# Hybrid decoder layer: two blocks of the latent branch's output projection computed as a pair with seven-product units

## The chip, the cores and the metric

The kernel runs on one core of a Trainium2 chip. The core has a matrix engine (TensorE, in the profile PE for matmuls and PEld for weight loads), a vector engine (DVE), a scalar engine (ACT), GpSimd (POOL) and SyncE (SP); the last two here mainly issue DMA transfers, which sixteen DMA engines carry out. Every engine works through its own list of instructions in order, and waits at an instruction until the semaphores it names have been reached. The metric is the device time of one execution in microseconds. Weights and activations lie in the chip's memory (HBM) and pass through on-chip memory; matmul results accumulate in eight banks of 128 x 512 numbers, here called accumulators.

## What is computed

One decoder layer on 256 tokens of width 2048, in float32:

```python
h  = rms_norm(x)
P  = h @ w_in                       # latent q, kv | rope key | windowed q, k, v | two gates
A  = latent attention (16 heads)    # o_a, 256 x 2048
B  = windowed attention (32 heads)  # o_b, 256 x 2048
merged = sigmoid(gA) * (A @ w_o_mla) + sigmoid(gB) * (B @ w_o_swa)
y  = merged @ w_out
x  = x + rms_norm(y)
a, b = split(rms_norm(x) @ w_up)    # 2 x 5632 columns
x  = x + rms_norm((gelu(causal_conv3(a)) * b) @ w_down)
```

The change concerns `A @ w_o_mla`, a product of 256 x 2048 by 2048 x 2048.

## The kernel before

**Products.** A float32 operand is held as two parts, hi (a cast to a reduced format, made by ACT) and lo (the remainder, made by DVE). `mm3` (L195 to L197) makes one product from three matmuls: hi by hi (L195), hi by the weight's lo (L196), lo by the weight's hi (L197). A weight chunk of 128 x 1024 comes by a DMA from SP into a raw buffer (`raw`), is cast (L160, `whi`) and has its remainder taken (L161, `wlo`). Raw buffers come from a ring of three with two more in some stages (`new_raw`), or in turn from a list of places (`more_raw`).

**Plain blocks.** `gemm` makes one block of 512 columns for both halves of the tokens, with two accumulators. It goes through the 16 pieces of 128 rows (k) of the weight; a chunk holds two of them, and gives 2 x 2 products, 12 matmuls.

**Pairs.** `pair_gemm` makes two blocks of 512 columns at once for both token halves, with four accumulators c. Its work is a row of units, each of two k, written as a string: "p" is plain, eight products; "s" forms the 2 x 2 x 2 block product with seven products from sums of weights and sums of activations. Three more intermediate sums go into four further accumulators q, and `end_sums` adds these together at the end. The sums of activations (`token_sums`) are made by DVE and ACT ahead of the unit. The differences of weights are either made on the spot or beforehand: `park_sums` loads two rows of weights through POOL into a staging tile (tag "sg"), lets DVE make four subtractions (L249) and writes both results to HBM, from where `seven_parked` loads them as ordinary chunks.

**Order.** The program counts ticks, one per chunk or unit half; `at(t, f)` puts a step into tick t. A scheduler then settles the order of each engine's list from what depends on what.

**Stages around the change.** The windowed branch comes first, then its gates and its projection; latent attention (heads in eight units); the last windowed block; the four blocks of the latent gates, whose tanh values ACT makes (L1005) and POOL stores to HBM as `ta_d` (L1006); then A @ w_o_mla (`wo_a`) as four plain blocks j, each evacuated by DVE with the gates loaded back (`merge_loads`, tiles `lta` and `lyb`: L1047 and L1048) and transposed by TensorE (`m_cols`). At the start of this stage memory areas of earlier stages are given back and opened anew as areas p3, p6, px and p4; a tile there waits for all that used the place before. Behind it stand W_out (a pair w of units "ppspspsp" and two plain blocks), the residual (x is loaded anew, `late_loads`, L1029), the up columns in eleven groups, with the down product as pairs d0, d1, db and dc between and after them. The last pair, dc, leaves its second token half partly to the end (`rest`). The tail squares and sums the result, scales it, adds the residual and stores it.

In before, the differences for dc (tc0 to tc3) and one set for the pairs d (ta4) are made during latent attention, seven sets (ta) in the up groups 1 to 5, and those for db (tb) in the groups 6 to 10. The four last additions of dc (L1472: the sums of the seven-product units to the down result `dsum`, in the profile ds) are put into ticks 16 and 17 after the end of db.

Of the kernel before, what the change touches and what calls it, by code (L numbers as in the profile page):

```python
# [11 lines left out]
F32 = mybir.dt.float32  # L12
F32R = mybir.dt.float32r
# [3 lines left out]
ALU = mybir.AluOpType  # L17
AX = mybir.AxisListType

P = 128  # L20
D = 2048
S = 256
NT = 2
KT = D // P
# [18 lines left out]
def trunk_layer(ctx, tc, x, x_cols_in, conv_cols_in, g_mix_post, g_ffn_post, w_in, w_q, w_kv,  # L43
                sinks, rel, wo_a, wo_b, w_out, w_up, w_down, rope_tab, strip_sel, out):
    nc = tc.nc
    vec, act, pe, pool = nc.vector, nc.scalar, nc.tensor, nc.gpsimd
# [29 lines left out]
    def warm_up(n):  # L76
        for i in range(n):
# [6 lines left out]
                       base=0, channel_multiplier=1)  # L84
# [20 lines left out]
    flex = ["raw"]  # L105
# [22 lines left out]
    def wchunk(src, shape, own=None, rawp=None, rbufs=1, parts=None):  # L128
        i = cnt[0]
        cnt[0] += 1  # L130
        n = int(np.prod(shape))
        raw = rawp.tile([P, 1024], F32, name=f"raw{i}", tag="xraw", bufs=rbufs) if rawp else \
            new_raw(f"raw{i}")
        dst = raw[:, :n]
        if len(shape) == 2:
            dst = dst.rearrange("p (a b) -> p a b", a=shape[0])
        elif len(shape) == 3:
            dst = dst.rearrange("p (a b c) -> p a b c", a=shape[0], b=shape[1])
        if len(shape) == 3:
            for k in range(shape[0]):  # L140
                nc.sync.dma_start(dst[:, k], src[:, k])
        else:
            ins = nc.sync.dma_start(dst, src)
            if more_raw and more_raw[-1] is raw_x and "rx" not in staged:
                staged.add("rx")
                tc.keep_in_program_order(ins)
        return convert(raw, n, own=own, parts=parts)

    def convert(raw, n, own=None, parts=None, into=None):
        i = cnt[0]  # L150
        cnt[0] += 1
        if into:
            hi, lo = into
        elif own:
            hi, lo = (own.tile([P, 1024], F32R, name=f"w{part}{i}", tag="w" + part) for part in ("hi", "lo"))
        else:
            extra = in_turn("w")
            hi, lo = (ring_tile("w" + part, f"w{part}{i}", F32R, extra) for part in ("hi", "lo"))
        for a, b in parts or ((0, n),):
            act.copy(hi[:, a:b], raw[:, a:b])  # L160
            vec.tensor_tensor(lo[:, a:b], raw[:, a:b], hi[:, a:b].bitcast(F32), op=ALU.subtract)  # L161
        return hi, lo
# [14 lines left out]
    def at(t, *fs):  # L177
        steps[max(t, now[0])].extend(fs)
# [55 lines left out]
    def park_sums(name, w, k, c0, pl, tag, t0, bufs=None):  # L234

        td = [dram.tile([P, 1024], F32, name=f"{name}{i}") for i in range(2)]
        st = []

        def load():
            st.append(sb(pl, [P, D], f"{name}s", tag=tag, bufs=bufs))  # L240
            for i in range(2):
                ins = pool.dma_start(st[0][:, i * 1024:(i + 1) * 1024], w[(k + i) * P:(k + i + 1) * P, c0:c0 + 1024])
                if tag not in staged:
                    tc.keep_in_program_order(ins)
            staged.add(tag)

        def less(o, x, y):
            o, x, y = (st[0][:, i * 512:(i + 1) * 512] for i in (o, x, y))
            tc.keep_in_program_order(vec.tensor_tensor(o, x, y, op=ALU.subtract))  # L249
# [12 lines left out]
        at(t0, even)  # L262
        at(t0 + 1, odd)
        return td

    def park_a(i, pl, tag, t0, **kw):
        u, p = (i, 0) if i < NA[0] else (i - NA[0], 1)
        return park_sums(f"ta{i}_", w_down, 2 * u, 1024 * p, pl, tag, t0, **kw)
# [717 lines left out]
        at(t0 + 6, lambda: pt(0), lambda: pt(1))  # L986
        at(t0 + 7, lambda: pv(0), lambda: pv(1))

    for i in range(NB2):
        parked_b2.append(park_sums(f"tc{i}_", w_down, 24 + 2 * i, 1024, t0=now[0] + 7 + 7 * i, **STAGE))  # L990
    parked_a.append(park_a(EARLY, t0=now[0] + 7 + 7 * NB2, **STAGE))
    b = now[0] + 2
    for u in range(8):
        if u % 4 == 0:
# [26 lines left out]
    def late_loads(i):  # L1021

        if i < 4:
            if i == 0:
                gpost.append(sb(p6, [P, D], "gpost", tag="gp"))
            pool.dma_start(gpost[0][:, i * 512:(i + 1) * 512], g_mix_post[i * 512:(i + 1) * 512].partition_broadcast(P))
        else:
            t, j = divmod(i - 4, 4)
            nc.sync.dma_start(x2[t][j], x[t * P:(t + 1) * P, j * 512:(j + 1) * 512])  # L1029
# [4 lines left out]
    def m_cols(p, ld):  # L1034
        pt = pst.tile([P, 512], F32, name=f"mT{p}", tag="t")
        for i in range(2):
            for t in range(NT):
                c = (2 * (p % 2) + i) * P
                pe.transpose(pt[:, i * 256 + t * P:i * 256 + (t + 1) * P], ld[t][0][:, c:c + P], ident)
        split_to(mth[p][:, :], mtl[p][:, :], pt, 0.5)  # L1040

    def merge_loads(j):
        ld = []
        for t in range(NT):
            a = sb(p4, [P, 512], f"lta{j}_{t}", tag="lta", bufs=3)
# [4 lines left out]
        return ld  # L1050

    yg_all = [[sb(p6, [P, 1024], f"yg_{t}_{j}", tag="f" + "ab"[t], bufs=2) for j in range(2)] for t in range(NT)]
# [7 lines left out]
    for i in range(4, 12):  # L1060
        at(now[0] + 10 + 2 * i, lambda i=i: late_loads(i))
    for j in range(4):
        ld = merge_loads(j)
        if j == 2:
            for u in range(W_ORDER.count("s")):
                at(now[0] + 2 + 4 * u, lambda u=u: m_sums(u))
        acc, _ = gemm(AH, AL, wo_a, 0, KT, 512 * j, 512, ps=(pss, "s") if j == 3 else None)
        for t in range(NT):
            a, b = ld[t]
            vec.scalar_tensor_tensor(a, a, 1.0, acc[t], op0=ALU.add, op1=ALU.mult)  # L1070
            vec.tensor_tensor(a, a, b, op=ALU.add)
        for p in range(2):
            at(now[0] + (2 if j == 3 else 1) + p, lambda p=2 * j + p, ld=ld: m_cols(p, ld))


    blocks = [(0, 512), (512, 512), (1024, 512), (1536, 256), (1792, 256)]
# [186 lines left out]
    def unpark(t, j):  # L1263
        if j == 0:
            x2_all[t] = sb(p3, [P, D], f"x2b_{t}", tag=f"x2_{t}")
        c = slice(j * 512, (j + 1) * 512)
        nc.sync.dma_start(x2_all[t][:, c], x2_d[t, :, c])
# [57 lines left out]
            at(now[0] + 1 + 2 * i, lambda i=i: conv_cols(4 * c + i, sa[0][i], sa[1][i], slot0 + i))  # L1325

    es7 = ffn_up0()
    for i in range(sum(NA) - EARLY - 1):
        parked_a.append(park_a(i + EARLY + 1, t0=now[0] + 8 + 15 * i // 2, **STAGE))
    for c in range(1, 6):  # L1330
        if c == 2:
            for i in range(8):
# [16 lines left out]
    def turn_flex(kind):  # L1349
        flex[0] = kind  # L1350
        turn.update(raw=0, w=0)

    f_raw = lambda n: lambda name: sb(p6, [P, 1024], name, tag="f" + n, bufs=2)

# [24 lines left out]
        sb_of[u] = token_sums(gtiles[u].bitcast(F32), a, m, hi, lo)  # L1379

    parked_b = [park_sums(f"tb{i}_", w_down, 24 + 2 * i, 0, t0=now[0] + 6 + 8 * i, **STAGE) for i in range(NB_)]
    for c in range(6, 11):
        if c == 6:
            at(now[0] + 1, x_raws)
        if c == 9:
            at(now[0] + 5, more_raw.clear)
            for u in range(NB_):
                at(now[0] + 2 + 4 * u, lambda u=u: b_sums(u))
        ffn_up(c, 4 * (c - 6))
# [77 lines left out]
        ud2[:] = [x_[:, j * 512:(j + 1) * 512] for x_ in (a_tile(f"ue{k}", k) for k in (4, 5)) for j in range(2)]  # L1467
        return ud2

    for i in range(4):  # L1470
        t, j = divmod(i, 2)
        at(now[0] + 16 + i // 2, lambda t=t, j=j, i=i: vec.tensor_tensor(dsum[t][2 + j], dsum[t][2 + j], ud2[i], op=ALU.add))  # L1472
    at(now[0] + 17, lambda: act.activation(first, ssz[1][:, 1:2], AF.Sqrt))
    more_raw[:] = [raw_of, f_raw("a"), raw_of, f_raw("b"), raw_of, f_raw("a"), raw_x, f_raw("b")]

# [8 lines left out]
                  into=held_into)  # L1484
    for i in range(8):
        unpark(i // 4, i % 4)
    z_block(c[0], 2, 0)
    z_block(c[1], 3, 0)
    z_pre(0)
# [24 lines left out]


RING = 4
GATE_ORDER = "psppspsp"
B_ORDER = "psspsspssp"
B2_ORDER = "ppsspssppp"
# [80 lines left out]
```

## Time and profile before

| | |
|---|---|
| time, median of 3 runs | 1459.37 us (1459.1 to 1459.7) |
| profiled execution | 1461.47 us, its span 1459.4 us |
| granted TensorE clock | 0.998 |
| TensorE busy | 1447.8 us, 99% |
| DVE busy | 1140.4 us, 78% |
| ACT busy | 858.0 us, 59% |
| DMA | 241 GB/s in the mean |
| latent attention, latent gates | up to 552.70 us |
| A @ wo_a, four plain blocks | 552.70 to about 640 us |
| W_out | about 640 to 724 us |
| residual, first up group | about 724 to 777 us |
| up groups 1 to 5 | 777 to 1000 us |
| pairs d0, d1 | 1000 to 1124 us |
| up groups 6 to 10 | 1124 to 1347 us |
| pairs db, dc | 1347 to about 1440 us |

The names in a profile line are those of the program without the buffers' numbers. A line of a timeline gives the start, the duration, the engine, the line of the program, the operation and, in square brackets, the engine's idle time before it with what ended that. Matmuls overlap: the interval between two starts, not the duration, is what one costs. DMA lines are given at their issue; the time to landing stands apart.

### The profile page before, as it was taken

Reading aid. Unit: us, or ns where it says so; the run is one execution under the profiler, and the core shown is the slowest. Engines: PE = TensorE matmul, PEld = TensorE weight load, DVE = VectorE, ACT = ScalarE, POOL = GpSimd, SP = SyncE. Lnnn points to the kernel's source line nnn. Section 1 sums busy time; section 2 is a strip of 40 time slices with the busy share of each in tenths; the row PEclk is TensorE's granted clock in tenths of the full one; section 3 lists DMA queues with packets and bytes.
Section 4 is the critical chain, followed back from the end, with each engine's and each line's share of the span. In section 5 each row is a group of like instructions: output and inputs, shape, how many; then the busy total and the mean of one; then the engine's idle time right before and its main releaser. Section 6 shows DMA issues by size and latency. Waiting matters only on the chain.

```text
span 1459.4 us, 21333 instructions
## 1 busy us (share of the span) xinstructions
PE 1447.8 (99%) x7531; PEld 1235.9 (85%) x7531; DVE 1140.4 (78%) x1990; ACT 858.0 (59%) x1412; POOL 107.2 (7%) x192
## 2 busy tenths in 40 slices
PE   9999999999999999999999999999999999999997
PEld 7888888888898888888888888888888888888886
DVE  7788896766778765768799899876778797876797
ACT  7588864544555654446576565655646565665673
POOL 0011110010000001100000011000000100000000
PEclk9999999999999999999999999999999999999999
DMA  8755376699775769864766888856988988667965
GB/s 295 216 164 169 109 260 188 221 322 293 246 216 176 238 226 345 261 200 168 227 207 209 267 313 299 280 174 210 312 271 267 313 270 292 197 188 252 347 218 195
DMA packets 164199, 351.08 MB, mean 241 GB/s; under 512 B 20555, under 2 KB 31724, under 8 KB 164092
## 3 DMA queue, kind: packets, MB, share of 16 engines
q1 hardware_dynamic: 144480, 280.40, 59.3%
q0 software_dynamic: 19520, 69.27, 14.1%
q8 instruction: 59, 0.97, 0.3%
q14 instruction: 48, 0.39, 0.1%
q10 hardware_dynamic: 92, 0.05, 0.0%
HBM read 318.16 MB, written 31.51 MB: 240 GB/s over the span
## 4 chain that ended last, share of the span: by engine, by line
PE 93%; DMA 3%; DVE 2%; ACT 1%; issue 1%; DVEq 0%; ACTq 0%
PE accg L195 10%; PE accg L197 10%; PE accg L196 10%; PE ub L1293 10%; PE ua L1293 10%; PE ub L1297 5%; PE ua L1297 5%; PE cd L195 2%; PE cd L196 2%; PE cd L197 2%; DVE wlo L161 1%; DMA raw<-in_ffn_w_down_dram 1%; PE cdb L196 1%; DMA raw<-in_w_out_dram 1%; PE mpo L977 1%; PE cdb L195 1%
## 5 line engine op out<-in xcount | busy, mean ns | idle before, releaser
L161 DVE TENSOR_TENSOR wlo<-raw,whi 128x1024 fp32r<-128x1024 f32 (+2 forms) x498 | 587.2, 1190 | 206.7 <-ACT whi L160 198.9
L160 ACT CAST whi<-raw 128x1024 fp32r<-128x1024 f32 (+2 forms) x498 | 505.0, 1024 | 384.4 <-PE accg L197 150.1
L195 PE MATMUL accg<-whi,ahl 128*128 128x512 f32 (+1 forms) x416 | 162.8, 391 | 0.0
L197 PE MATMUL accg<-whi,ahl 128*128 128x512 f32 (+1 forms) x416 | 160.6, 386 | 0.0
L196 PE MATMUL accg<-wlo,ahl 128*128 128x512 f32 (+1 forms) x416 | 159.8, 384 | 0.0
L1293 PE MATMUL ub<-ahl,whi 128*128 128x512 f32 x640 | 154.7, 391 | 0.0
L1293 PE MATMUL ua<-ahl,whi 128*128 128x512 f32 x640 | 154.6, 391 | 0.0
L1293 PEld LDWEIGHTS ub<-ahl,whi 128*128 128x128 f32 x640 | 117.5, 188 | 22.9 <-ACT cc L1185 0.3
L1293 PEld LDWEIGHTS ua<-ahl,whi 128*128 128x128 f32 x640 | 117.5, 188 | 22.7
L195 PE MATMUL accg<-whi,bhl 128*128 128x512 f32 x320 | 125.6, 392 | 0.0
L197 PE MATMUL accg<-whi,bhl 128*128 128x512 f32 x320 | 124.8, 390 | 0.0
L196 PE MATMUL accg<-wlo,bhl 128*128 128x512 f32 x320 | 124.7, 390 | 0.0
L197 PEld LDWEIGHTS accg<-whi,ahl 128*128 128x128 f32 x416 | 78.1, 188 | 15.5
L196 PEld LDWEIGHTS accg<-wlo,ahl 128*128 128x128 f32 x416 | 78.2, 188 | 13.1
L195 PEld LDWEIGHTS accg<-whi,ahl 128*128 128x128 f32 x416 | 78.2, 188 | 12.9
L1297 PEld LDWEIGHTS ub<-ahl,wlo 128*128 128x128 f32 x640 | 82.3, 191 | 3.3
L1297 PEld LDWEIGHTS ua<-ahl,wlo 128*128 128x128 f32 x640 | 82.2, 191 | 3.1
L1297 PE MATMUL ua<-ahl,wlo 128*128 128x256 f32 x640 | 83.7, 283 | 0.0
L1297 PE MATMUL ub<-ahl,wlo 128*128 128x256 f32 x640 | 83.3, 283 | 0.0
L197 PEld LDWEIGHTS accg<-whi,bhl 128*128 128x128 f32 x320 | 60.1, 188 | 12.6
L196 PEld LDWEIGHTS accg<-wlo,bhl 128*128 128x128 f32 x320 | 60.1, 188 | 12.1
L195 PEld LDWEIGHTS accg<-whi,bhl 128*128 128x128 f32 x320 | 60.1, 188 | 12.1
(610 smaller groups left out, 2534.9 us busy)
## 6 DMA issues: line engine op xcount, KB each, us to landing
raw<-in_ffn_w_up_dram SPq DMA_DIRECT2D x142, 512.0 KB, 4.6
raw<-in_w_in_dram SPq DMA_DIRECT2D x105, 512.0 KB, 4.6
raw<-in_ffn_w_down_dram SPq DMA_DIRECT2D x66, 512.0 KB, 5.7
xraw<-in_ffn_w_up_dram SPq DMA_DIRECT2D x34, 512.0 KB, 5.1
raw<-in_w_o_swa_dram SPq DMA_DIRECT2D x32, 512.0 KB, 5.1
raw<-in_w_o_mla_dram SPq DMA_DIRECT2D x32, 512.0 KB, 5.6
raw<-in_w_out_dram SPq DMA_DIRECT2D x26, 512.0 KB, 4.2
ta_s<-in_ffn_w_down_dram POOLq DMA_DIRECT2D x24, 512.0 KB, 6.5
```

Source lines behind the costliest of these rows:

```text
L160: act.copy(hi[:, a:b], raw[:, a:b])
L161: vec.tensor_tensor(lo[:, a:b], raw[:, a:b], hi[:, a:b].bitcast(F32), op=ALU.subtract)
L195: pe.matmul(o, ah, bh, start=start, stop=False)
L196: pe.matmul(o, ah, bl, start=False, stop=False)
L197: pe.matmul(o, al, bh, start=False, stop=stop)
L977: pe.matmul(o, w(t), p_[:, c], start=n == 0, stop=n == 5)
L1293: pe.matmul(acc[i], hi[:, c], hn[p][:, j * 512:(j + 1) * 512], start=p + j == 0, stop=stop)
L1297: pe.matmul(acc[i][:, 0:256], lo[:, c], hn[p][:, j * 512:j * 512 + 256], start=False, stop=False)
```

## The change

The first two blocks of A @ wo_a are computed as a pair of units "ppspspsp" in place of two plain blocks: five plain units and three with seven products. Each of the three takes its weight differences from HBM (tw0 to tw2). They are made during latent attention in the place of tc1 to tc3 and ta4; ta4 moves into the up groups 1 to 5, and tc1 to tc3 into the groups 6 to 10. The sums of A's tokens are made by `a_sums` into tiles `as0` and `as1`, which lie in the places of the x tiles to be loaded later, with rx as scratch. The raw buffers of the pair go in turn through seven places, two of which are halves of a new tile `araw` in area p6. The pair's c takes the four accumulators of the plain blocks, its q the four others; so block 2 now uses the accumulators pss and block 3 the others. The loads of x come later, and the gates of block 1 get tiles of their own (`la1`, `lb1`). Last, the four additions of dc are written behind the unparking in place of the ticks 16 and 17.

```diff
+    as_ = {}
+    as_tiles = []
+
+    def a_sums(u):
+        if u % 2 == 0:
+            as_tiles.append(sb(p3, [P, D], f"as{u // 2}", F32R, tag=f"x2_{u // 2}"))
+        o = u % 2 * 1024
+        tmp = sb(base, [P, 1024], f"at{u}", tag="rx")
+        as_[u] = token_sums(at_[u].bitcast(F32), tmp[:, 0:512], tmp[:, 512:1024],
+                            as_tiles[u // 2][:, o:o + 512], as_tiles[u // 2][:, o + 512:o + 1024])
+
+    def merged(a, b, acc):
+        vec.scalar_tensor_tensor(a, a, 1.0, acc, op0=ALU.add, op1=ALU.mult)
+        vec.tensor_tensor(a, a, b, op=ALU.add)
...
+    def a_pair():
+        halves = [sb(p6, [P, 1024], f"l{n}1", tag="f" + n, bufs=2) for n in "ab"]
+        lds = [merge_loads(0), [[x_[:, t * 512:(t + 1) * 512] for x_ in halves] for t in range(NT)]]
+        for t in range(NT):
+            for x_, src in zip(lds[1][t], (ta_d, yb_d)):
+                pool.dma_start(x_, src[1, t])
+        gp = sb(p6, [P, D], "araw", tag="gp")
+        more_raw[:] = [raw_of, raw_f, raw_of, lambda name: gp[:, 0:1024], raw_of, raw_f, lambda name: gp[:, 1024:2048]]
+        c = pair_gemm("a", wo_a, 0, 0, A_ORDER, lambda k, t: (AH(k)[:, t * P:(t + 1) * P], AL(k)[:, t * P:(t + 1) * P]),
+                      lambda u: as_[u], 0, ud_place, parked=parked_w)
+        more_raw.clear()
+        turn.update(raw=0)
...
+    for u in range(NA_):
+        at(now[0] + 3 * u, lambda u=u: a_sums(u))
+    for i in range(4, 12):
+        at(now[0] + 20 + 2 * i, lambda i=i: late_loads(i))
+    turn_flex("raw")
+    a_pair()
...
-    for i in range(NB2):
-        parked_b2.append(park_sums(f"tc{i}_", w_down, 24 + 2 * i, 1024, t0=now[0] + 7 + 7 * i, **STAGE))
-    parked_a.append(park_a(EARLY, t0=now[0] + 7 + 7 * NB2, **STAGE))
+    parked_w = [park_sums(f"tw{i}_", wo_a, 2 * i, 0, t0=now[0] + 7 + 7 * i, **STAGE) for i in range(NA_)]
+    parked_b2.append(park_sums("tc0_", w_down, 24, 1024, t0=now[0] + 7 + 7 * NA_, **STAGE))
...
-    for i in range(sum(NA) - EARLY - 1):
-        parked_a.append(park_a(i + EARLY + 1, t0=now[0] + 8 + 15 * i // 2, **STAGE))
+    for i in range(sum(NA) - EARLY):
+        parked_a.append(park_a(i + EARLY, t0=now[0] + 8 + 15 * i // 2, **STAGE))
...
+    for i in range(1, NB2):
+        parked_b2.append(park_sums(f"tc{i}_", w_down, 24 + 2 * i, 1024, t0=now[0] + 6 + 8 * NB_ + 15 * (i - 1) // 2, **STAGE))
...
-    for i in range(4):
-        t, j = divmod(i, 2)
-        at(now[0] + 16 + i // 2, lambda t=t, j=j, i=i: vec.tensor_tensor(dsum[t][2 + j], dsum[t][2 + j], ud2[i], op=ALU.add))
...
     for i in range(8):
         unpark(i // 4, i % 4)
+    for i in range(4):
+        t, j = divmod(i, 2)
+        vec.tensor_tensor(dsum[t][2 + j], dsum[t][2 + j], ud2[i], op=ALU.add)
...
+A_ORDER = "ppspspsp"
+NA_ = A_ORDER.count("s")
```

Three places show what this does to the order on the engines. Lines past 148 have numbers higher by 4 in after. The first place is SP's list where the projection's chunks are loaded, with the semaphores that each issue waits for (DMAHW for transfers issued by SP, DMASW for those issued by POOL). Before, with in_w_o_mla as wo_a and x2 as the tile of x:

```order
L143 DMA raw358_6083<-in_w_o_mla_dram 128x2x512 [waits DMAHW3_49,DVE_49]
L143 DMA raw360_6101<-in_w_o_mla_dram 128x2x512 [waits DMAHW4_49,DVE_49]
L143 DMA raw362_6133<-in_w_o_mla_dram 128x2x512 [waits DMAHW5_49,DVE_49]
L1029 DMA x2_0_5950<-in_x_dram 128x512 [waits DMASW3_49,DMASW4_49,DMASW2_49,DMASW5_49,DMASW1_49,DMASW6_49,DMASW0_49,DMASW7_49,PE_49,Pool_49]
L143 DMA raw364_6151<-in_w_o_mla_dram 128x2x512 [waits DMAHW6_49,DVE_49]
```

After, at the same place:

```order
L172 DMA raw360_6093<-tw0_1_3733 128x1024 [waits DMAHW3_49,DMASW0_49,DVE_49]
L172 DMA raw362_6105<-in_w_o_mla_dram 128x1024 [waits DMAHW2_49,DVE_49]
L172 DMA raw364_6132<-in_w_o_mla_dram 128x1024 [waits DMAHW4_49,DVE_49]
L172 DMA araw_5964<-in_w_o_mla_dram 128x1024 [waits DMASW3_49,DMASW4_49,DMASW2_49,DMASW5_49,DMASW1_49,DMASW6_49,DMASW0_49,DMASW7_49,Activation_49,Pool_49]
L172 DMA araw_5964<-tw0_0_3732 128x1024
```

The eight waits for POOL's transfers, which stood at the first load of x, now stand at the first load into araw. That load brings the fourth chunk that TensorE uses; the three ahead of it in the list belong to later units.

The second place is TensorE's list at that fourth chunk (whi353 and wlo353 in both). Before:

```order
L197 MATMUL accg_346_1_5974<-whi351_6013,bhl2_4158 128x512
L195 MATMUL accg_346_0_5973<-whi353_6031,bhl3_4159 128x512
L196 MATMUL accg_346_0_5973<-wlo353_6032,bhl3_4159 128x512
L197 MATMUL accg_346_0_5973<-whi353_6031,bhl3_4159 128x512
L195 MATMUL accg_346_1_5974<-whi353_6031,bhl3_4159 128x512
```

After, where ca are the pair's c and qa its q:

```order
L201 MATMUL ca_3_5968<-whi351_6016,bhl4_4158 128x512
L199 MATMUL ca_0_5965<-whi353_6033,bhl4_4158 128x512
L199 MATMUL ca_1_5966<-whi353_6033,bhl4_4158 128x512
L199 MATMUL ca_2_5967<-whi353_6033,bhl4_4158 128x512
L199 MATMUL ca_3_5968<-whi353_6033,bhl4_4158 128x512
L199 MATMUL qa_0_6057<-whi357_6075,bhl0_4154 128x512
L200 MATMUL ca_0_5965<-wlo353_6034,bhl4_4158 128x512
L201 MATMUL ca_0_5965<-whi353_6033,bhl4_4158 128x512
```

The four hi products of the chunk, and one of a chunk two places further on, now stand ahead of the first product with its lo half.

The third place is DVE's list at the end of the last pair dc, where ue are the sums of its seven-product units, ds the down result, and cdc the pair's c. Before:

```order
L161 TENSOR_TENSOR wlo1087_14290<-raw1086_14287,whi1087_14289 128x1024
L356 TENSOR_TENSOR ue5_14226<-ue5_14226,qdc_1_14010 128x512
L357 TENSOR_TENSOR ue4_14225<-ue4_14225,qdc_1_14010 128x512
L1472 TENSOR_TENSOR ds1_7716<-ds1_7716,ue5_14226 128x512
L1472 TENSOR_TENSOR ds0_7715<-ds0_7715,ue4_14225 128x512
L1472 TENSOR_TENSOR ds1_7716<-ds1_7716,ue5_14226 128x512
L161 TENSOR_TENSOR wlo1089_14302<-raw1088_14299,whi1089_14301 128x1024
L1398 TENSOR_TENSOR ds0_7715<-ds0_7715,cdc_0_13917 128x512
```

After:

```order
L165 TENSOR_TENSOR wlo1099_14379<-raw1098_14376,whi1099_14378 128x1024
L360 TENSOR_TENSOR ue5_14319<-ue5_14319,qdc_1_14103 128x512
L361 TENSOR_TENSOR ue4_14318<-ue4_14318,qdc_1_14103 128x512
L165 TENSOR_TENSOR wlo1101_14391<-raw1100_14388,whi1101_14390 128x1024
L1534 TENSOR_TENSOR ds0_7764<-ds0_7764,ue4_14318 128x512
L1534 TENSOR_TENSOR ds1_7765<-ds1_7765,ue5_14319 128x512 x2
L1446 TENSOR_TENSOR ds0_7764<-ds0_7764,cdc_0_14010 128x512
```

The last weight conversion has moved ahead of the three additions that stood before it; the additions now stand directly ahead of the first step of the tail.

More of the change, by code (lines that the diff above doesn't have):

```diff
@@ L147, in wchunk, with turn_flex @@
         return convert(raw, n, own=own, parts=parts)
+    def turn_flex(kind):
+        flex[0] = kind
+        turn.update(raw=0, w=0)
     def convert(raw, n, own=None, parts=None, into=None):
@@ L1044, in merge_loads @@
         for t in range(NT):
[L1045 removed]
+            a = sb(p4, [P, 512], f"lta{j}_{t}", tag="lta", bufs=4)
             b = sb(p4, [P, 512], f"lyb{j}_{t}", tag="lyb", bufs=2)
@@ L1050, in merge_loads, with ud_place, pair_evac @@
         return ld
+    as_ = {}
[10 more added lines that the diff above has]
+        vec.tensor_tensor(a, a, b, op=ALU.add)
+    ud_a = []
+    def ud_place():
+        d = sb(base, [P, D], "uda", tag="sg")
+        ud_a[:] = [d[:, j * 512:(j + 1) * 512] for j in range(4)]
+        return ud_a
+    def a_pair():
[10 more added lines that the diff above has]
+        turn.update(raw=0)
+        def pair_evac(i):
+            t, j = divmod(i, 2)
+            vec.tensor_tensor(ud_a[i], ud_a[i], c[i], op=ALU.add)
+            merged(*lds[j][t], ud_a[i])
+        for n_, i in enumerate((0, 2, 1, 3)):
+            at(now[0] + n_, lambda i=i: pair_evac(i))
+        for p in range(4):
+            at(now[0] + 3 + p, lambda p=p: m_cols(p, lds[p // 2]))
+    for u in range(NA_):
[4 more added lines that the diff above has]
+    a_pair()
     yg_all = [[sb(p6, [P, 1024], f"yg_{t}_{j}", tag="f" + "ab"[t], bufs=2) for j in range(2)] for t in range(NT)]
@@ L1058, in m_sums @@
         ms[u] = token_sums(mt[u].bitcast(F32), yg[0][0], yg[0][1], st[:, 0:512], st[:, 512:1024])
-    for i in range(4, 12):
-        at(now[0] + 10 + 2 * i, lambda i=i: late_loads(i))
-    for j in range(4):
+    for j in range(2, 4):
         ld = merge_loads(j)
-        if j == 2:
+        if j == 3:
             for u in range(W_ORDER.count("s")):
-                at(now[0] + 2 + 4 * u, lambda u=u: m_sums(u))
-        acc, _ = gemm(AH, AL, wo_a, 0, KT, 512 * j, 512, ps=(pss, "s") if j == 3 else None)
+                at(now[0] + 1 + 3 * u, lambda u=u: m_sums(u))
+        acc, _ = gemm(AH, AL, wo_a, 0, KT, 512 * j, 512, ps=(pss, "s") if j == 2 else None)
         for t in range(NT):
-            a, b = ld[t]
-            vec.scalar_tensor_tensor(a, a, 1.0, acc[t], op0=ALU.add, op1=ALU.mult)
-            vec.tensor_tensor(a, a, b, op=ALU.add)
+            merged(*ld[t], acc[t])
         for p in range(2):
-            at(now[0] + (2 if j == 3 else 1) + p, lambda p=2 * j + p, ld=ld: m_cols(p, ld))
+            at(now[0] + 2 + p, lambda p=2 * j + p, ld=ld: m_cols(p, ld))
     blocks = [(0, 512), (512, 512), (1024, 512), (1536, 256), (1792, 256)]
@@ L1347, in down @@
         return gemm(xh, xl, w_down, k0, nk, c0, n, split=split, ps=ps)
-    def turn_flex(kind):
-        flex[0] = kind
-        turn.update(raw=0, w=0)
     f_raw = lambda n: lambda name: sb(p6, [P, 1024], name, tag="f" + n, bufs=2)
@@ L1486, in trunk_layer @@
         unpark(i // 4, i % 4)
+    for i in range(4):
+        t, j = divmod(i, 2)
+        vec.tensor_tensor(dsum[t][2 + j], dsum[t][2 + j], ud2[i], op=ALU.add)
     z_block(c[0], 2, 0)
```

## The prediction

> **What bounds the kernel now.** I read the page first, then the busy time by stretches of the program, then the waits where the change works.
>
> ```profile
> span 1459.4 us, 21333 instructions
> PE 1447.8 (99%) x7531; PEld 1235.9 (85%) x7531; DVE 1140.4 (78%) x1990; ACT 858.0 (59%) x1412; POOL 107.2 (7%) x192
> PE 93%; DMA 3%; DVE 2%; ACT 1%; issue 1%; DVEq 0%; ACTq 0%
> ```
>
> The second line is busy time, the third the shares of the chain that ended last. TensorE is the bound nearly everywhere, so a matmul that disappears is worth its interval, and any wait of TensorE is lost in full. Where it waits shows in the table by stretches:
>
> ```profile
> core 0: us, PE busy (x) PEld busy (x) DVE busy (x) ACT busy (x) POOL busy (x), PEclk, DMA share, GB/s
> 230.00:552.70 322.70, 322.70 (x1757) 278.06 (x1756) 228.18 (x359) 165.89 (x252) 31.67 (x59) 1.00 0.75 240
> 552.70:640.00 87.30, 87.30 (x398) 72.21 (x397) 57.32 (x71) 37.98 (x42) 9.65 (x18) 1.00 0.85 289
> 777.00:1000.00 223.00, 223.00 (x1291) 197.08 (x1290) 185.39 (x317) 130.92 (x214) 14.94 (x28) 1.00 0.78 259
> 1124.00:1347.00 223.00, 223.00 (x1284) 197.03 (x1283) 178.92 (x294) 126.01 (x199) 12.82 (x24) 1.00 0.77 249
> 1347.00:1440.00 93.00, 92.46 (x406) 75.45 (x404) 79.03 (x94) 60.43 (x77) 0.00 (x0) 1.00 0.82 285
> 1440.00:1459.40 19.40, 10.65 (x54) 8.97 (x54) 14.28 (x36) 4.08 (x14) 0.00 (x0) 0.88 0.29 109
> ```
>
> The rows are: latent attention with its gates; the output projection A @ wo_a (first matmul at 552.70); the two stretches of up columns; the last pairs; the tail. In the first four TensorE has no idle time to win back. The projection also runs with the DMA engines 85% busy, so it has no idle transfer time to spare either.
>
> **Fewer matmuls.** Three units of the pair use seven products in place of eight, each product three matmuls of 128x512: 3 x 3 = 9 fewer. The interval comes from the first and the twentieth matmul of the stage:
>
> ```profile
> 552.70 0.39 PE L195 MATMUL accg<-whi,bhl 128*128 128x512 f32 x1
> ...
> 557.01 0.39 PE L196 MATMUL accg<-wlo,bhl 128*128 128x512 f32 x1
> ```
>
> 4.31 us for 19 intervals: 0.227 us. 9 x 0.227 = **-2.04 us**, all of it on the path.
>
> **The fourth weight chunk (a new wait).** In before, wo_a arrives through a ring whose buffers come free one by one, and nine chunk loads were issued by 556 (the first row below). The only load here that goes into freshly opened memory is x, and nothing on TensorE needs it soon. In after, the fourth chunk goes into the new tile araw, which lies in that memory too. Its issue takes over the eight DMA waits that x has in before, among them the landing of the last two stores of the gates:
>
> ```profile
> 528.04 28.14 SPq L143 DMA_DIRECT2D raw<-in_w_o_mla_dram  x9
> ...
> 553.21 1.23 POOL L1006 DMA_DIRECT2D ta_d<-ta  x2 [2.85 <-ACT ta L1005]
> ...
> SPq L1029 <- DMA ta_d<-ta: 2.7, 1, 2.7
> ...
> 559.17 0.34 SPq L1029 DMA_DIRECT2D x<-in_x_dram  x1
> 559.61 0.38 SPq L143 DMA_DIRECT2D raw<-in_w_o_mla_dram  x1
> ```
>
> After the nine loads come the stores, SP's wait for them, and SP's first issues behind it. So araw is issued at about 559.17. Its rivals for bandwidth there are of the same kind as x's (512 KB pieces from SP, loads from POOL). Landing times, in this order: the x issue at 559.17 (256 KB); the raw at 559.61 (512 KB); all raws of 535 to 572 with the conversions that follow:
>
> ```profile
> DMA to landing us min/median/max: 3.9/3.9/3.9
> ...
> DMA to landing us min/median/max: 5.6/5.6/5.6
> ...
> L160 ACT CAST whi<-raw x13: 1037/1055/1055, 535.0 to 571.9; 128x1024 fp32r<-128x1024 f32 x13
> L161 DVE TENSOR_TENSOR wlo<-raw,whi x12: 1215/1224/1226, 536.3 to 570.3; 128x1024 fp32r<-128x1024 f32 x12
> ...
> DMA to landing us min/median/max: 4.8/6.8/9.8
> ```
>
> I take 4.8, between x's 3.9 (same place in the queue, half the bytes) and the 5.6 of the raw right behind it. The chunk lands at 563.97, its ACT cast ends at 565.02. TensorE is through the three chunks before it at 552.70 + 36 x 0.227 = 560.87. It then has four hi products of the chunk, up to 561.78 if nothing were late, and as the fifth one of the first difference product, whose weights ACT casts two places further back: after a whole chunk (1.05) and a half one, priced here by the half-width row
>
> ```profile
> L160 ACT CAST whi<-raw 128x512 fp32r<-128x512 f32 x26 | 16.0, 621 | 7.3 <-PE cd L197 4.0 <-DMA raw<-in_w_in_dram 2.1 <-DMA raw<-in_ffn_w_down_dram 0.8
> ```
>
> at 0.62: 566.69, with 0.05 for the hand-over 566.74. Stall: 566.74 - 561.78 = 4.96, **+5.0 us**. The chunk's lo half (1.22 on DVE, done at 566.24) comes before that. What stands ahead of that lo half on DVE, the token sums of the first seven-product unit, waits for the same stores; by the rows
>
> ```profile
> L374 DVE TENSOR_TENSOR sba<-bhl 128x512 f32<-128x512 f32 x6 | 4.1, 686 | 0.0
> L414 DVE TENSOR_TENSOR sb<-sbm,sb 128x512 fp32r<-128x512 f32 x6 | 4.1, 685 | 0.1
> L378 DVE TENSOR_TENSOR sbm<-sba 128x128 f32<-128x128 f32 x6 | 1.7, 285 | 0.0
> ```
>
> it is 2 x 0.685 + 2 x 0.686 + 4 x 0.29 = 3.9 us plus two casts on ACT between (1.37 for two pieces of that size would be ta's price), from 559.1 to 564.4: 0.6 before DVE could start the lo half. That cover is thin, but it holds.
>
> Bounds of the stall: x's 3.9 instead of 4.8 gives 4.1; the median 6.8 gives 7.0, the longest 9.8 gives 10.0. The stores themselves could land sooner than here, where the second, issued near 553.9, held SP until 559.1. Issue to landing of all eight of L1006:
>
> ```profile
> DMA to landing us min/median/max: 2.7/5.1/6.7
> ```
>
> With 2.7 and 3.9 together only 1.6 is left; nothing excludes it, but the DMA engines are as loaded as in before.
>
> The Trainium skill ("DMA: Bandwidth & Descriptors", Anatomy of one DMA) gives a transfer from GpSimd about 2.0 us plus its bytes at 436 GB/s. By that, as an estimate, 512 KB would land 3.2 us after issue, the stall would be 3.4 and the sum 1.6 lower. The trace does not agree: x, half that size and first in its queue, took 3.9.
>
> The next chunks then come in time: three were loaded before the stop, and araw's other half goes out right behind its first. DVE's next three lo halves (1.22 + 0.68 + 1.22) are done at 569.4; TensorE asks for the last of them 18 matmuls after 566.74, at 570.8.
>
> **The last sums.** In before, DVE makes three of the four additions on the second down pair ahead of the last weight conversion, and TensorE waits for that conversion:
>
> ```profile
> 1437.12 0.68 DVE L357 TENSOR_TENSOR ue<-ue,qdc 128x512 f32<-128x512 f32 x1
> 1437.72 1.89 DVE L1472 TENSOR_TENSOR ds<-ds,ue 128x512 f32<-128x512 f32 x3
> 1439.52 1.22 DVE L161 TENSOR_TENSOR wlo<-raw,whi 128x1024 fp32r<-128x1024 f32 x1
> 1441.57 0.69 DVE L1398 TENSOR_TENSOR ds<-ds,cdc 128x512 f32<-128x512 f32 x1 [0.83 <-PE cdc L197]
> ...
> 1449.33 0.69 DVE L1506 TENSOR_TENSOR ds<-ds,cdc 128x512 f32<-128x512 f32 x1
> 1450.40 0.42 DVE L1398 TENSOR_TENSOR z<-ds,zb 128x256 f32<-128x256 f32 x1 [0.39 <-PE zb L197]
> ...
> 1439.08 0.39 PE L195 MATMUL cdc<-wh,bhl 128*128 128x512 f32 x1
> 1440.79 0.50 PE L196 MATMUL cdc<-wlo,ghl 128*128 128x512 f32 x1 [1.33 <-DVE wlo L161]
> ```
>
> In after the conversion starts at 1437.72 and TensorE has it at 1438.99, before it asks at 1439.31: its stall of 1.48 goes. DVE then makes the three additions (to 1440.7) and is late next: the first z addition starts at 1440.7 instead of 1441.57, a gain of 0.87, and from there DVE is busy up to the last z blocks. At 1450.40 it waited 0.39 more for TensorE, which is now 1.48 earlier. Gain: 0.87 + 0.39 = **-1.26 us** at the end. Bounds: 0.87 (if that second wait stays) and 1.48.
>
> **What costs nothing.** Seven-product units need their differences made beforehand. Latent attention makes one such set fewer, the first up stretch one more, the second up stretch three more, each four subtractions:
>
> ```profile
> L249 DVE TENSOR_TENSOR tb_s<-tb_s 128x512 f32<-128x512 f32 x24 | 16.4, 685 | 0.1
> ```
>
> 12 x 0.685 = 8.2 us more on DVE in 223, which takes its 178.92 to 187.1. The first up stretch has 185.39 in before with TensorE busy throughout; that is the cover, and if it failed, DVE's lo halves would come late by a part of 0.69 each. The POOL transfers for these sets go beside an SP queue at 0.77 load. The pair's evacuation (one copy and eight additions more) lies beside the next block's 96 matmuls; the x loads moved later are needed only after W_out.
>
> **Sum.** -2.04 + 5.0 - 1.26 = +1.7 us. The profiled execution took 1461.47 us, 2.1 above the median of the runs, 1459.37; all terms are differences, so I add them to the median: **1461.1 us** (+0.12%). A measurement of this kernel can tell about 0.2% (2.9 us) from no change, so this is "within 0.2%".
>
> **The rivals.** (a) *The fourth chunk is not late.* Only the two gains stay: -3.3 us, 1456.1, faster. Place: araw's issue. It decides if the stall is under 0.4, which with a landing of 4.8 needs the stores down by 554.6, 0.7 us after the second's issue; no store of the eight was as quick (2.7). A stall between 0.4 and 6.2 ends within 0.2%.
>
> (b) *The idle TensorE comes back slow.* At the start of the program its matmuls run slowly at first:
>
> ```profile
> 5.70:11.00 5.30, 5.30 (x14) 1.00 0.87 284
> 11.00:20.00 9.00, 9.00 (x41) 1.00 0.99 362
> ```
>
> The columns are time, TensorE's busy time and matmuls, granted clock, DMA share and rate. 14 took 0.379 each, later ones 0.220, with a granted clock of 1.00 in both. If a stop of 5 us (the four hi products in its midst make it 4.1 and 0.8) brings that back for as many, it costs up to 14 x 0.159 = 2.2 us: +3.9, 1463.3, slower. Against it: the 1.33 us of idle in the tail brought nothing of it, but no row of before has a long idle stretch in the middle. The Trainium skill ("TensorE: Matmul & The Clock Gate", Part 1: The HAM clock gate) says that the array drops to half rate after a whole idle window of about 3.4 us, the windows running free; a stop of 4.1 would hold a whole one about one time in five.
>
> (c) *The chunk lands at the usual pace of this stretch.* With 6.8 us the stall is 7.0 and the time 1463.1; with 9.8 it is 1466.1; from 6.0 on it is slower. For it: the DMA share of 0.85; against: it is first in its queue.
>
> (d) *The tail gains nothing*, because its end hangs on DVE or the last stores: 1462.3, at the edge of what can be told. For it: DVE is busy for 14.28 of the last 19.40 us; against: both of DVE's waits there were for TensorE.
>
> (e) *Parked sums make DVE late* in the second up stretch: four or five lo halves late by 0.69 give some 3 us, 1464.1, slower. Against it is the fuller first up stretch, without a wait.
>
> **How the numbers follow.** The forecast, with stalls of 4 to 6 us (1460.2 to 1462.2), has 0.43; (d) 0.10, half of it on each side of the bound; (a) 0.12, (b) 0.13, (c) 0.15, (e) 0.07. Faster: 0.12. Slower: (b), (c), (e) and half of (d), 0.40. Same: 0.48. The range runs from 1456.8, which leaves (a) out, to 1464.4, which leaves out the long landings of (c) and the worse half of (e), together some 0.2.
>
> **What the profile after would show.** TensorE idle about 4 us near 561, after 36 matmuls of the stage, on a hi product released by an ACT cast of araw, and 0.8 us four matmuls later; SP issuing araw behind the gate stores; nine matmuls fewer; no stall of TensorE on a lo half near 1439; up stretches still at full busy share. Wrong it would be if araw landed before 561, or if TensorE showed idle time in the pair's later units, where I count on about 1 us of slack.

## The result, and the profile after

| | before | after |
|---|---|---|
| time, median of 12 runs | 1459.78 us (1458.78 to 1461.56) | 1463.31 us (1461.67 to 1464.37) |
| ratio | | 1.0022, 95% interval 1.0013 to 1.0031 |
| profiled execution | 1461.47 us, span 1459.4 us | 1462.59 us, span 1460.8 us |
| matmuls and transposes of TensorE | 7531 | 7522 |

The change makes the kernel slower by 3.5 us between the medians; the interval of the ratio is 1.9 to 4.5 us. The two profiled executions lie closer together, because that of before was 1.7 us above its median and that of after 0.7 below; places are therefore compared one by one.

The chain that ended last, in order of time, names the new wait among its longest pieces:

```profile
553.03 5.26 DMA ta_d<-ta
558.56 4.42 DMA araw<-in_w_o_mla_dram
```

The second store of the gates takes from 553.03 to 558.3, the fourth chunk from 558.56 to 563.0. The waits of SP and the lists of ACT and TensorE around it say the same:

```profile
SPq L172 <- DMA ta_d<-ta: 6.2, 2, 5.7
...
558.39 0.62 ACT L417 CAST as<-at 128x512 fp32r<-128x512 f32 x1 [5.66 <-DMA ta_d<-ta]
561.55 0.62 ACT L417 CAST as<-at 128x512 fp32r<-128x512 f32 x1 [2.54 <-DVE at L384]
563.01 1.04 ACT L164 CAST whi<-araw 128x1024 fp32r<-128x1024 f32 x1 [0.84 <-DMA araw<-in_w_o_mla_dram]
...
551.85 0.39 PE L199 MATMUL ca<-whi,bhl 128*128 128x512 f32 x1
...
559.78 0.39 PE L201 MATMUL ca<-whi,bhl 128*128 128x512 f32 x1
564.11 2.07 PE L199 MATMUL ca<-whi,bhl 128*128 128x512 f32 x4 [3.94 <-ACT whi L164]
565.98 0.63 PE L199 MATMUL qa<-whi,bhl 128*128 128x512 f32 x1
566.40 0.63 PE L200 MATMUL ca<-wlo,bhl 128*128 128x512 f32 x1
...
569.36 0.39 PE L201 MATMUL ca<-whi,bhl 128*128 128x512 f32 x1
569.59 0.40 PE L199 MATMUL ca<-whi,bhl 128*128 128x512 f32 x1
```

ACT waits 5.7 us at the token sums for the same stores, then for DVE, then for the chunk. TensorE, which had started the stage at 551.85, stands still from 560.0 to 564.1. And behind that its matmuls are slow: from 564.11 to about 569.2 they start every 0.43 us instead of every 0.227. The table by stretches shows it in the granted clock (columns: the stretch, its length, TensorE's busy time and matmuls, clock, DMA share, GB/s):

```profile
552.00:560.00 8.00, 8.00 (x37) 1.00 0.68 241
560.00:564.11 4.11, 0.17 (x2) 0.80 0.95 318
564.11:569.36 5.25, 5.25 (x12) 0.50 0.94 285
569.36:580.00 10.64, 10.64 (x48) 1.00 0.85 289
```

The clock was halved. The matmul at 569.59 is the fiftieth of the stage; without a loss it would have started 49 x 0.2268 us after 551.85, at 562.96. The place costs 6.6 us: 4.1 us standing still and 2.5 us of slow matmuls.

At the end, DVE's list reads as the order foretold; the last line here is before's last results, for comparison:

```profile
1439.56 0.69 DVE L361 TENSOR_TENSOR ue<-ue,qdc 128x512 f32<-128x512 f32 x1
1440.15 1.23 DVE L165 TENSOR_TENSOR wlo<-raw,whi 128x1024 fp32r<-128x1024 f32 x1
1441.29 1.90 DVE L1534 TENSOR_TENSOR ds<-ds,ue 128x512 f32<-128x512 f32 x3
1443.09 0.69 DVE L1446 TENSOR_TENSOR ds<-ds,cdc 128x512 f32<-128x512 f32 x1
...
1454.92 2.74 DVE L1480 SCALAR_TENSOR_TENSOR ds<-ds,rz,x2b 128x512 f32<-128x512 f32 x4
...
1453.61 2.74 DVE L1432 SCALAR_TENSOR_TENSOR ds<-ds,rz,x2b 128x512 f32<-128x512 f32 x4
```

From the same step (L357 before, L361 after) to the last results it takes 1454.92 - 1439.56 = 15.36 us; before it took 1453.61 - 1437.12 = 16.49. That is 1.1 us less. TensorE has no wait there any more, nor in the up stretches, in which DVE has grown:

```profile
777.00:1000.00 223.00, 223.00 (x1284) 196.96 (x1283) 189.53 (x324) 131.62 (x216) 17.07 (x32) 1.00 0.81 266
1124.00:1347.00 223.00, 223.00 (x1278) 196.80 (x1277) 187.97 (x307) 126.74 (x199) 19.25 (x36) 1.00 0.84 278
1347.00:1440.00 93.00, 93.00 (x419) 77.27 (x418) 77.41 (x92) 61.95 (x79) 0.00 (x0) 1.00 0.85 291
```

Together: 9 matmuls fewer, -2.0; the fourth chunk, +6.6; the end, -1.1 to -1.5 (what DVE gains, and the 1.48 that TensorE's wait cost); sum +3.1 to +3.5, against 3.5 measured. In the profiles the stage alone, from its first matmul to the first of W_out, grew from 89.96 us (552.70 to 642.66) to 94.59 (551.85 to 646.44), by 4.6: the first two terms together.

### The profile page after: what moved, and what is told of

The parts are those of the page before. It is cut to its first block, busy times and chain, and to the rows that moved or that the text cites. A ratio compares the mean times of both kernels' runs of the same rounds, so it can differ in the third digit from the quotient of the medians.

```text
span 1460.8 us, 21421 instructions
## 1 busy us (share of the span) xinstructions
PE 1446.8 (99%) x7522; PEld 1235.8 (85%) x7522; DVE 1163.0 (80%) x2034; ACT 865.5 (59%) x1422; POOL 113.6 (8%) x204
## 4 chain that ended last, share of the span: by engine, by line
PE 58%; DVE 2%; DMA 1%; issue 1%; ACT 0%; DVEq 0%; SPq 0%; ACTq 0%
PE ua L1343 10%; PE ub L1343 10%; PE ua L1347 5%; PE ub L1347 5%; PE accg L201 3%; PE accg L199 3%; PE accg L200 3%; PE cd L200 2%; PE cd L199 2%; PE cd L201 2%; PE cdb L200 1%; PE cdb L201 1%; PE cdb L199 1%; PE cw L199 1%; PE cw L201 1%; PE cw L200 1%
## 5 line engine op out<-in xcount | busy, mean ns | idle before, releaser
L199 PE MATMUL accg<-whi,bhl 128*128 128x512 f32 x256 | 100.7, 393 | 0.0
L201 PE MATMUL accg<-whi,bhl 128*128 128x512 f32 x256 | 100.0, 390 | 0.0
L200 PE MATMUL accg<-wlo,bhl 128*128 128x512 f32 x256 | 99.8, 390 | 0.0
L201 PEld LDWEIGHTS accg<-whi,bhl 128*128 128x128 f32 x256 | 48.1, 188 | 10.2
L200 PEld LDWEIGHTS accg<-wlo,bhl 128*128 128x128 f32 x256 | 48.1, 188 | 9.6
L199 PEld LDWEIGHTS accg<-whi,bhl 128*128 128x128 f32 x256 | 48.1, 188 | 9.6
```

Source lines behind the costliest of these rows:

```text
L199: pe.matmul(o, ah, bh, start=start, stop=False)
L200: pe.matmul(o, ah, bl, start=False, stop=False)
L201: pe.matmul(o, al, bh, start=False, stop=stop)
```

## The experiments

Two theories were open after this. Mine: the whole loss is one late transfer, the chunk that goes into reopened memory, plus a slow clock that follows from it. The rival: the pair is too tight as such, and would lose its time somewhere even without that wait. For the slow matmuls there was a second pair: a clock that falls after idle time, or contention when all engines start again together.

**Five raw places, no araw.** The pair's buffers go through the ring alone.

```diff
-        gp = sb(p6, [P, D], "araw", tag="gp")
-        more_raw[:] = [raw_of, raw_f, raw_of, lambda name: gp[:, 0:1024], raw_of, raw_f, lambda name: gp[:, 1024:2048]]
+        more_raw[:] = [raw_of, raw_f, raw_of, raw_of, raw_f]
```

> The pair's raw buffers go through the five ring places only; the tile araw is gone, all else as in after. Theory (the fourth chunk's wait for the gate stores, and the slow matmuls behind it, are the loss): no idle time of TensorE near 560 us and no slow matmuls there, 6.6 us less in that place. The sums of the first seven-product unit still wait for the same stores on ACT and DVE, so 1 to 2 us should stay at that unit's difference chunks. Time 4.6 to 5.6 us under after, about 1458.2 us, 1.5 under before. Rival (the pair itself is too tight for its transfers, and five places make it worse): idle time of TensorE spread over the later units, more than 2 us in all, time not under before.

Measured: 1457.88 us, 5.4 under after, ratio to before 0.9985 (0.9976 to 0.9993; before 1459.93). The stop near 560 and the slow matmuls are gone. What stays are short waits for lo halves in the first seven-product unit, the longest two being

```profile
565.84 0.50 PE L200 MATMUL qa<-wlo,as 128*128 128x512 f32 x1 [0.28 <-DVE wlo L165]
...
567.91 0.50 PE L200 MATMUL qa<-wlo,as 128*128 128x512 f32 x1 [0.41 <-DVE wlo L165]
...
560.00:572.00 12.00, 11.22 (x47) 1.00 0.91 307
```

By the last line 47 matmuls start between 560 and 572, where 53 would at 0.227: some 1.3 us lost. They come where the token sums, held up by the same stores, crowd DVE. The loss of the change was the wait, and not the pair.

**Eight matmuls more in the stop.** Work without use, so that TensorE stands still for a shorter time:

```diff
+                if name == "a" and k == 2 * NA_ + 2:
+                    after_three[:] = [w_]
+                if name == "a" and k == 2 * NA_ + 3:
+                    q[:] = banks(1 - kind, f"q{name}_")
+                    wf = after_three[0]
+                    for f in range(FILL):
+                        tc.keep_in_program_order(pe.matmul(q[0], act_of(k - 1, 0)[0], half(wf, 0)[0], start=True, stop=True))
...
+FILL = 8
```

> After, with eight more matmuls of 128x512 on data already there, put between the third and the fourth chunk of the pair (their result is overwritten by the first product into that accumulator, so only time is added). They take 1.8 us out of the idle stretch of 4.1 us. Theory A (the array runs slowly after the stop because it had been idle for more than some 3 us): every matmul behind the stop has an interval of 0.227 us, the 2.5 us of slow ones are gone; a new wait of about 1 us on the chunk's lo half, which the slow matmuls hid, comes in; time 1.5 us under after (1 to 2.5). Theory B (they are slow because all engines start again at once on the same memory): 12 to 13 matmuls with 0.427 us remain, time at or above that of after.

Measured: 1464.12 us, 0.8 above after, which six runs from 1461.33 to 1465.87 do not tell from no change. Neither theory had it right: slow matmuls remain, but not at the restart. The stop is now in two pieces (the scheduler has also put three of the four hi products behind the first lo product, so that the lo half is waited for), and the clock still falls:

```profile
565.43 0.50 PE L199 MATMUL ca<-whi,bhl 128*128 128x512 f32 x1 [2.56 <-ACT whi L164]
566.69 0.50 PE L200 MATMUL ca<-wlo,bhl 128*128 128x512 f32 x1 [0.76 <-DVE wlo L165]
...
560.90:565.43 4.53, 1.98 (x9) 1.00 0.93 290
565.43:567.26 1.83, 1.07 (x3) 1.00 0.97 383
567.26:570.66 3.40, 3.40 (x10) 0.50 0.97 252
570.66:580.00 9.34, 9.34 (x42) 1.00 0.85 248
```

But it falls 1.8 us after the restart, and for 3.4 us. Contention at the restart would slow the first matmuls. A clock that looks back over fixed windows of 3.4 us would do just this: in the window before, 563.86 to 567.26, TensorE had worked for about 1 us. One that looks back over a sliding 3.4 us would have fallen sooner: the 3.4 us up to the restart at 565.43 held only 0.9 us of work. After fits as well: looked at in steps of 0.2 us, its clock is low from about 562.5 to 569.3, twice 3.4, and in the window ahead, 559.1 to 562.5, TensorE had worked for 1.1 us.

**Sixteen matmuls more.** The same edit with `FILL = 16`.

> As the one with eight extra matmuls, but sixteen (3.6 us), which leaves two idle stretches of about 0.9 us each in the stop. There slow matmuls stayed with eight, for 3.4 us, but began only 1.8 us after the restart. Theory A, mended (the clock looks at fixed windows of some 3.4 us and slows the next one if a window was mostly idle; a stop of 2.6 and one of 0.8 in one window are enough): with sixteen no window is mostly idle, every matmul near 565 to 572 us has 0.227 us, and the place costs 5.5 us in place of 6.7, time 1.1 us under after. Theory B (slow because all engines restart together): some 8 to 13 matmuls with 0.427 us remain, time 0.6 us or more above after.

Measured: 1461.95 us, 1.4 under after, ratio to before 1.0015 (1.0006 to 1.0024; before 1460.04).

```profile
560.14 3.79 PE L298 MATMUL qa<-whi,bhl 128*128 128x512 f32 x16
564.11 0.50 PE L199 MATMUL ca<-whi,bhl 128*128 128x512 f32 x1 [0.19 <-ACT whi L164]
565.37 0.50 PE L200 MATMUL ca<-wlo,bhl 128*128 128x512 f32 x1 [0.76 <-DVE wlo L165]
...
560.14:565.37 5.23, 4.29 (x18) 1.00 0.96 336
565.37:572.00 6.63, 6.63 (x29) 1.00 0.91 292
```

TensorE's list differs from that with eight by the eight matmuls alone. Every engine restarts as before at 564.1, the DMA share is as high, and no matmul is slow: the mended theory A holds. What this is worth is less certain. In the profiled executions the stage, up to the first matmul of W_out, takes 93.06 us (551.98 to 645.04) against 94.59 in after, 1.5 less; the 1.4 between the medians says the same, but the intervals of the two ratios overlap.

**The last additions back.**

```diff
+    for i in range(4):
+        t, j = divmod(i, 2)
+        at(now[0] + 16 + i // 2, lambda t=t, j=j, i=i: vec.tensor_tensor(dsum[t][2 + j], dsum[t][2 + j], ud2[i], op=ALU.add))
...
-    for i in range(4):
-        t, j = divmod(i, 2)
-        vec.tensor_tensor(dsum[t][2 + j], dsum[t][2 + j], ud2[i], op=ALU.add)
```

> After, with the four additions of the last pair back at the ticks 16 and 17. Theory: TensorE waits 1.3 to 1.5 us for the last lo half again, DVE has it 1.9 us later, and the time is 1.3 us above after (0.9 to 1.6). Rival (the end hangs on DVE or the last stores): the wait comes back, the time stays within 0.5 us of after.

Measured: 1465.55 us (1463.11 to 1468.8), 2.2 above after. The wait on the last lo half is back (first two lines):

```profile
1445.80 0.39 PE L199 MATMUL cdc<-wh,bhl 128*128 128x512 f32 x1
1447.37 0.50 PE L200 MATMUL cdc<-wlo,ghl 128*128 128x512 f32 x1 [1.18 <-DVE wlo L165]
...
1362.95 0.50 PE L199 MATMUL cdb<-whi,bhl 128*128 128x512 f32 x1 [1.39 <-ACT whi L164]
1364.22 0.50 PE L200 MATMUL cdb<-wlo,bhl 128*128 128x512 f32 x1 [0.76 <-DVE wlo L165]
```

The profiled execution also has waits near 1360, on chunks that landed late; the engines' lists are the same as in after up to the tail, so that differs from one execution to the next. The runs spread over 5.7 us, and the size of the tail is better taken from the next one.

The same equality makes this a second look at after's stop. TensorE waits 3.8 us near 560 for the same chunk, but the clock is low for one stretch of 3.4 us, from 564.94, and not for two:

```profile
558.11:561.52 3.41, 1.78 (x8) 1.00 0.63 150
561.52:564.94 3.42, 1.20 (x4) 1.00 1.00 395
564.94:568.35 3.41, 3.21 (x8) 0.50 0.81 254
```

A window with 1.20 us of work brought the low clock on, the one ahead of it with 1.78 had not. How the stop lies to the windows thus decides what it costs.

**The last additions alone.** Before, with only that part of the change.

> Before, with only the four additions of the last pair written behind the unparking; no pair in A @ wo_a, no sets moved. Theory: the last lo half moves ahead of three additions, TensorE's wait of 1.3 to 1.5 us near 1439 goes, time 1.26 us under before (0.9 to 1.5), ratio 0.9991. Rival (the end hangs on DVE or the last stores): the wait goes and the time stays within 0.4 us of before.

Measured: 1458.72 us against 1460.04, 1.3 less; the ratio, 0.9994 with 0.9985 to 1.0003, does not by itself exclude no change. The mechanism is there: the lo half starts at 1435.70, ahead of the three additions,

```profile
1435.11 0.68 DVE L357 TENSOR_TENSOR ue<-ue,qdc 128x512 f32<-128x512 f32 x1
1435.70 1.23 DVE L161 TENSOR_TENSOR wlo<-raw,whi 128x1024 fp32r<-128x1024 f32 x1
1436.84 1.89 DVE L1486 TENSOR_TENSOR ds<-ds,ue 128x512 f32<-128x512 f32 x3
1438.65 0.69 DVE L1398 TENSOR_TENSOR ds<-ds,cdc 128x512 f32<-128x512 f32 x1
```

and the first addition of the tail follows L357 by 3.54 us, against 4.45 in before. The two opposite edits, at +2.2 and -1.3, point the same way, but neither is clear of the spread of its runs: the moved conversion and the vanished wait are shown, a gain of about 1.1 to 1.3 us is what they make likely.

**The sums elsewhere too.** Five places, and the token sums in the activation tiles that the gates have just left, so that nothing in the pair waits for the stores.

```diff
-        if u % 2 == 0:
-            as_tiles.append(sb(p3, [P, D], f"as{u // 2}", F32R, tag=f"x2_{u // 2}"))
-        o = u % 2 * 1024
         tmp = sb(base, [P, 1024], f"at{u}", tag="rx")
-        as_[u] = token_sums(at_[u].bitcast(F32), tmp[:, 0:512], tmp[:, 512:1024],
-                            as_tiles[u // 2][:, o:o + 512], as_tiles[u // 2][:, o + 512:o + 1024])
+        as_[u] = token_sums(at_[u].bitcast(F32), tmp[:, 0:512], tmp[:, 512:1024], mt[7 - u][:, 0:512], mt[7 - u][:, 512:1024])
...
-        gp = sb(p6, [P, D], "araw", tag="gp")
-        more_raw[:] = [raw_of, raw_f, raw_of, lambda name: gp[:, 0:1024], raw_of, raw_f, lambda name: gp[:, 1024:2048]]
+        more_raw[:] = [raw_of, raw_f, raw_of, raw_of, raw_f]
```

> As the one with five places, and the sums of A's tokens go into the activation tiles that the latent gates have just finished with (mt 7, 6, 5) in place of the x tiles, so that neither a chunk nor the sums wait for the gate stores. Theory: TensorE has no idle time above 0.5 us in the pair; what is left of the change is nine matmuls fewer (2.0 us) and the tail (1.3 us): time 3.3 us under before, about 1456.5 us, ratio 0.9977. Rival (five places are too few, or the longer DVE list makes lo halves late): 1 us or more of idle time left in the later units.

Measured: 1465.27 us, ratio 1.0041 (1.0029 to 1.0053). The theory missed; idle time in a later unit came, as the rival had it, but not from the causes that it named. TensorE now waits later, 0.8 us and then 4.4 us on chunks that landed late, and pays the slow clock again:

```profile
580.86 0.80 PE L199 MATMUL qa<-whi,ahl 128*128 128x512 f32 x1 [4.36 <-ACT whi L164]
...
579.76 1.04 ACT L164 CAST whi<-raw 128x1024 fp32r<-128x1024 f32 x1 [4.76 <-DMA raw<-tw]
...
SPq L1032 <- DMA ta_d<-ta: 6.1, 2, 5.5
...
L1032 SPq DMA_DIRECT2D x<-in_x_dram x8: 328/457/771, 558.2 to 592.0; - x8
...
DMA to landing us min/median/max: 5.9/9.9/12.7
```

The last three lines are SP's wait at the x loads, the x loads, and the landings of the pair's chunks issued from 555 to 580. In after, the sums lay in the x tiles and so held the x loads back until 586. With the sums gone the scheduler let those loads out between the weight chunks. The first of them waits up to 5.5 us for the same gate stores and holds up the chunks behind it in SP's list; from 558.2 on six of them go out among the chunks, and these took up to 12.7 us to land.

**x held back.** The same, with the x loads pinned to their place in the program; only SP's list differs.

```diff
-            nc.sync.dma_start(x2[t][j], x[t * P:(t + 1) * P, j * 512:(j + 1) * 512])
+            tc.keep_in_program_order(nc.sync.dma_start(x2[t][j], x[t * P:(t + 1) * P, j * 512:(j + 1) * 512]))
```

> As the one with the sums in the activation tiles, but the loads of x are pinned to the place in the program where they are written, behind the pair. Theory (that one lost its time because the x loads, no longer held back by the sums in their tiles, went out at 558 to 566 us and made weight chunks land 12 us after their issue): landings of the pair's chunks back at 4 to 7 us, no idle time of TensorE above 0.5 us in the pair, time 3.3 us under before, about 1456.6 us, ratio 0.9977. Rival (the sums made early make the DVE list too long, or five places are too few): the wait of 4.4 us near 580 stays, time above before.

Measured: 1456.86 us, ratio 0.9972 (0.9963 to 0.9980; before 1460.04), 3.2 us under before and 6.5 under after. The x loads go from 609.5 on, the chunks land in 3.3 to 8.0 us, and the only wait of TensorE in the stage is

```profile
PE qa L200 <- DVE wlo L165: 0.2, 1, 0.2
...
DMA to landing us min/median/max: 3.3/5.7/8.0
```

This version beats both kernels, and before by what the forecast gave the change without the chunk's wait (3.3). It takes away both what SP waited for at the x loads (the chunks now go out from 555.70) and their traffic; which of the two cost more stays open.

## Why the prediction was right, and where it was off

**Forecast and range.** 1463.31 lies in the range, near its upper end. The forecast, +1.7 within 0.2%, was short; +3.5, a slowdown at the edge of what can be told, is what rival (b) gave (+3.9, 1463.3). The number lies in the range because the range took in that rival, and not because the forecast's sum held.

**Nine matmuls, -2.0.** Right: the counts differ by nine, and the last version, without the wait, is faster by what the matmuls and the tail together were to give.

**The fourth chunk.** The mechanism was right in each part: SP issued araw behind the gate stores, at 558.56, 6.7 us after the stage began (forecast 6.5); it landed in 4.4 us (4.8); TensorE stood still for 4.1 us after 36 matmuls (4.15). The second stop, 0.8 us at the first difference product, did not appear: the hi products ahead of it ran at half rate, and its weights were ready in that time.

**The step that failed** is the term's size. It was +5.0; measured is 6.6. I had left the slow clock to a rival at 0.13, reasoning that a whole idle window had to fit into the stop, which gave one time in five. The runs show another condition: a window in which TensorE works for about 1 us of 3.4 is enough (eight matmuls more, the last additions back, and after itself). Of a stop of 4.1 us at least half falls into one window, which leaves it 1.4 us of work at most, an estimate from these two lengths; so such a stop will nearly always bring the slow clock on. The runs agree: the mean granted clock is 0.996 in all twelve of after, against 0.998 or 0.999 in every run of before beside the experiments. The price of that rival, 2.2 us from the matmuls at the program's start, was close to the 2.5 measured. That my row there has a granted clock of 1.00 is no measurement: the first clock record of the trace of before lies at 10.96 us, that of after at 9.52, and just there the matmuls turn fast. The start is thus likely the same slow clock.

**The last sums, -1.26.** The mechanism was right: the conversion moved ahead and the wait went. The size fits, 1.1 from the profiled executions and 1.3 from the edit alone, whose interval still includes no change.

**What costs nothing.** Right: DVE has 187.97 us in the second up stretch (forecast 187.1) with TensorE busy throughout; rival (e) did not come. Nothing was seen of (a) or (d). The one thing I had not priced is the crowding of DVE at the first unit; in after the stop hides it, with five places it shows as some 1.3 us.

**The loads of x.** That the x loads go later was counted as free. It was more than that: the last two versions differ in SP's list alone, and by 8.4 us, because the loads carry the wait for the gate stores and their own traffic into the pair.

## What to carry to other kernels

A tile in reopened memory waits for whatever used the place last, stores included; before giving such a tile an early use, look up in the trace when those stores land, and give the first loads a place that comes free by reading instead. When a wait on TensorE nears 3 us, add the slow clock to its price: here 3.4 or 6.8 us at half rate, part of it hidden in the stop. And a transfer that something happens to hold back may be better held back: when a dependency goes, see which loads it lets out.

## What the runs showed of the hardware that was not expected

The granted clock fell to 0.50 for one stretch of 3.41 us or for two: two in after (562.48 to 569.31, of which 1.6 fell into the stop) and with the sums elsewhere (578.75 to 585.58), one with eight matmuls more (567.26 to 570.68) and with the last additions back (564.94 to 568.35). The stretches lie on a fixed grid: in after the clock comes back at 569.31 and falls again, behind the last matmul, at 1456.78, which is 260 stretches of 3.413 us later.

The 3.41 us ahead of such a fall held 0.94 to 1.20 us of TensorE's work, by busy times whose ends are modelled. After windows of the grid with 1.78 us (the last additions back) and 1.59 (five places, 1447.07 to 1450.48) the clock stayed at 1.00, so the bound lies between 1.2 and 1.6 us. Once low, it stayed low after a window with 1.79 us of slow work (after) and came back after one with 3.21 (the last additions back).

The Trainium skill ("TensorE: Matmul & The Clock Gate", Part 1: The HAM clock gate) speaks of free-running windows of about 3.4 us and half rate after an idle one; length and rate agree, but the window need not be idle throughout.

Landing times of 512 KB chunks of the pair, issued between 555 and 580, ranged from 3.3 us (x held back) to 12.7 (six x loads among them).
